# A chunked delta rule on TensorE: chunks of 128 tokens, one head per product, against chunks of 64 tokens, four heads in step

## The chip, the cores and the metric

The kernel runs on one core of a Trainium2 chip. The metric is device time in microseconds (us); the figure for the kernel before is the median of three executions. A core has a matrix engine (TensorE, in the profile PE, with its weight loads as PEld), VectorE (DVE), ScalarE (ACT), GpSimd (POOL) and SyncE (SP), which here issues DMAs. Products accumulate in PSUM, whose banks hold 128 x 512 floats; everything else that is on chip lies in SBUF.

## The reference

One block of a language model for 512 tokens and a model width of 1024, in float32: a projection of the normalised input, two mixers (a gated delta rule with 8 heads, `dk` = 128 and `dv` = 256, and a retention with 4 heads), their gates, an output projection and an MLP of width 4096. The change concerns the delta rule:

```python
CHUNK = 64
g_cum = jnp.cumsum(g, axis=-1)
decay = jnp.exp(jnp.where(causal, g_cum[..., :, None] - g_cum[..., None, :], -jnp.inf))
lower = jnp.where(strict, jnp.einsum('bhncd,bhnmd->bhncm', k * beta[..., None], k) * decay, 0.0)
t_inv = lax.linalg.triangular_solve(lower, eye, left_side=True, lower=True, unit_diagonal=True)
u = jnp.einsum('bhncm,bhnme->bhnce', t_inv, v * beta[..., None])
w = jnp.einsum('bhncm,bhnmd->bhncd', t_inv, k * beta[..., None] * jnp.exp(g_cum)[..., None])
attn = jnp.where(causal, jnp.einsum('bhncd,bhnmd->bhncm', q, k) * decay, 0.0)
q_exp = q * jnp.exp(g_cum)[..., None]
k_dec = k * jnp.exp(g_last - g_cum)[..., None]
def step(state, inp):                       # one chunk; scanned over the sequence
    qe, ww, uu, aqk, kd, ld = inp
    v_new = uu - ww @ state
    o = qe @ state + aqk @ v_new
    state = state * ld + kd.T @ v_new
    return state, o
oa = rmsnorm(o, norm_a) * silu(za)
ya = oa @ w_br_a
```

The length of a chunk is a choice of the algorithm and changes nothing but rounding: the kernel before uses 128 tokens, the reference 64.

## The kernel before

**Products.** The large projections run in F32R, TensorE's faster format for 32-bit data. Each operand is split into a high and a low part, and a product is taken as three (high by high, high by low, low by high). Weights come by DMA in pieces of 512 KB and are split in SBUF by ACT (high part, L148) and DVE (low part, L149). The small products of the delta rule are plain F32, for which the profile shows two passes each. For part of the projections a scheme with seven products of quarter matrices in place of eight is used. It needs sums of weight blocks, which small background DMA jobs prepare while the kernel runs; `REST` and two more constants say by the program's own reckoning from when and how often such a job is issued, and a sum that isn't done when it is wanted is issued there and then.

**Layout of the delta rule.** `kf` and `qf` hold keys and queries with features on partitions, `kd` keys with tokens on partitions, `dall` the decays (later the attention matrix), `rt` the inverse of the triangular matrix, `vt` the values with tokens on partitions. A tile holds 128 tokens of one head, so nearly every product uses the whole array of 128 x 128.

**Stages of the delta rule.** `key_tile` finishes the keys of a head; `keys_chain` multiplies keys by keys and scales by the gates; `base_inverse` inverts blocks of 32 x 32 on DVE; `double_blocks` (L1080 to L1173) grows them to 64 and then to 128 with products in parts of the array: its helper `abreast` interleaves two or three streams of products that sit in different quadrants. `recurrence(g2)` (L1323) handles two heads. For each of four chunks it runs, with two products of 256 columns each: `ks` (keys by state), `qs` (queries by state), `px` (inverse by corrected values), `pc` (keys by new values, which updates the state) and `po` (attention by new values). Between them DVE corrects the values (L1339) and updates the state (L1364), and ACT scales out of PSUM (L1355). Four such pairs of heads follow each other. `gate_chain` then applies norm and gate to the outputs, transposes them and splits them for the product with `w_br_a` (`ya_filler`). `late_gates_filler` computes half of the gates by the seven-product scheme, with tokens on partitions.

**What sets the order.** The class `Clock` (L659 to L735) plans the program in advance. *Fillers* are the projections (values, queries, gates, `ya`), cut into pieces of a few products; *chains* are the steps above. A chain gives up control with the time after which it should go on (`KS_US`, `PX_US`, `PC_US` and others), and the planner puts filler pieces there until that time is reached by its own reckoning. Every product of this stage goes through `clock.matmul` (L668) or `clock.transpose` (L677), which pin it in program order, so the order on TensorE is exactly the planned one and a product that waits holds back all behind it. DVE and ACT work is ordered by priorities (`REC_PRIO`, `OUT_PRIO`).

**Banks.** The projections use four PSUM banks (`mm`), the transposes one, and the chains share a ring of three:

```python
def chain_bank():
    return psx.tile([P, 4, P], F32, tag="dl", name="dl", bufs=3)
```

The functions that the change touches, before it:

## Time and profile before

| | |
|---|---|
| median of three executions | 1327.68 us (1327.45 to 1330.72) |
| the profiled execution | 1326.62 us, its span 1324.8 us |
| PE busy | 1308.9 us, 99% |
| PEld busy | 1085.9 us, 82% |
| DVE busy | 931.3 us, 70% |
| ACT busy | 668.7 us, 50% |
| POOL busy | 89.7 us, 7% |
| granted clock of TensorE | 0.999 |

How to read the profile. Times are microseconds of one execution. A line such as `L668 PE MATMUL dl<-vt,kd 128*128 128x256 f32 x48 | 12.5, 383` names the source line, the engine, the operation, output and inputs by their names in the program, for TensorE the part of the array used (128*128 is all of it, rows by columns), the shape, the type and the number of instructions, then busy time and mean nanoseconds of one; what follows is idle time ahead of them and what ended it. In a timeline a line begins with start and duration. Matmuls are pipelined and their ends are modelled, so durations overlap; distances between starts are the safer figure.

### The profile page before, as it was taken

Reading aid. Unit: us, or ns where it says so; the run is one execution under the profiler, and the core shown is the slowest. Engines: PE = TensorE matmul, PEld = TensorE weight load, DVE = VectorE, ACT = ScalarE, POOL = GpSimd, SP = SyncE. Lnnn points to the kernel's source line nnn. Section 1 sums busy time; section 2 is a strip of 40 time slices with the busy share of each in tenths; the row PEclk is TensorE's granted clock in tenths of the full one; section 3 lists DMA queues with packets and bytes.
Section 4 is the critical chain, followed back from the end, with each engine's and each line's share of the span. In section 5 each row is a group of like instructions: output and inputs, shape, how many; then the busy total and the mean of one; then the engine's idle time right before and its main releaser. Section 6 shows DMA issues by size and latency. Waiting matters only on the chain.

```text
span 1324.8 us, 17530 instructions
## 1 busy us (share of the span) xinstructions
PE 1308.9 (99%) x6591; PEld 1085.9 (82%) x6591; DVE 931.3 (70%) x1560; ACT 668.7 (50%) x1168; POOL 89.7 (7%) x95
## 2 busy tenths in 40 slices
PE   9999999999999999999999999999999999999997
PEld 7888787888888878888888888888889888888886
DVE  6889757486666578876567776789685746637478
ACT  5784546455534533544453443465266636355364
POOL 2100100000000001000010000000001000000001
PEclk9999999999999999999999999999999999999999
DMA  5336952476765568887293462545629895859635
GB/s 192 134 112 160 203 132 64 114 181 174 191 161 133 127 178 179 271 253 153 79 260 105 120 214 64 160 157 175 223 82 247 230 256 156 245 154 251 191 119 135
DMA packets 115557, 223.16 MB, mean 168 GB/s; under 512 B 6982, under 2 KB 38896, under 8 KB 114960
## 3 DMA queue, kind: packets, MB, share of 16 engines
q1 hardware_dynamic: 96496, 175.13, 41.3%
q0 software_dynamic: 16944, 40.54, 19.1%
q10 hardware_dynamic: 2032, 6.36, 1.3%
q8 instruction: 52, 0.85, 0.3%
q14 instruction: 33, 0.27, 0.1%
HBM read 216.75 MB, written 72.37 MB: 218 GB/s over the span
## 4 chain that ended last, share of the span: by engine, by line
PE 89%; DVE 6%; ACT 3%; issue 1%; DMA 1%; DVEq 0%; ACTq 0%
PE mm L668 18%; PE mm L317 17%; PE dl L317 11%; PE mm L93 10%; PE mm L95 10%; PE mm L94 10%; PE dl L668 5%; PE tr L397 1%; DVE wlo L149 1%; PE dl L94 1%; PE dl L95 1%; PE dl L93 1%; PE tr L677 1%; PE mm L632 1%; DVE tmp L1061 1%
## 5 line engine op out<-in xcount | busy, mean ns | idle before, releaser
L149 DVE TENSOR_TENSOR wlo<-raw,whi 128x1024 fp32r<-128x1024 f32 x269 | 328.2, 1222 | 204.2 <-ACT whi L148 203.1
L148 ACT CAST whi<-raw 128x1024 fp32r<-128x1024 f32 x269 | 282.6, 1052 | 356.5 <-PE mm L668 71.7
L668 PE MATMUL mm<-actT,whi 128*128 128x512 f32 x448 | 144.5, 403 | 0.0
L317 PE MATMUL mm<-whi,xsum 128*128 128x512 f32 x384 | 120.6, 390 | 0.0
L95 PE MATMUL mm<-hn,wlo 128*128 128x512 f32 (+1 forms) x288 | 105.4, 366 | 0.0
L94 PE MATMUL mm<-hn,whi 128*128 128x512 f32 (+1 forms) x288 | 105.3, 366 | 0.0
L93 PE MATMUL mm<-hn,whi 128*128 128x512 f32 (+1 forms) x288 | 105.3, 366 | 0.0
L668 PEld LDWEIGHTS mm<-actT,whi 128*128 128x128 f32 x448 | 80.6, 188 | 14.8
L668 PE MATMUL mm<-actT,wlo 128*128 128x512 f32 x224 | 87.7, 392 | 0.0
L317 PEld LDWEIGHTS mm<-whi,xsum 128*128 128x128 f32 x384 | 71.8, 188 | 14.9
L317 PE MATMUL mm<-wlo,xsum 128*128 128x512 f32 x192 | 74.8, 390 | 0.0
L317 PE MATMUL dl<-whi,ffq 128*128 128x512 f32 x224 | 71.3, 389 | 0.0
L668 PE MATMUL mm<-whi,og 128*128 128x512 f32 x192 | 62.3, 397 | 0.0
L95 PEld LDWEIGHTS mm<-hn,wlo 128*128 128x128 f32 x288 | 54.3, 189 | 8.8
L93 PEld LDWEIGHTS mm<-hn,whi 128*128 128x128 f32 x288 | 54.3, 189 | 8.7
L94 PEld LDWEIGHTS mm<-hn,whi 128*128 128x128 f32 x288 | 54.3, 189 | 8.7
L668 PE MATMUL mm<-whi,actT 128*128 128x512 f32 x176 | 60.3, 405 | 1.0 <-DVE qf L906 1.0
L317 PE MATMUL dl<-whi,actT 128*128 128x512 f32 x192 | 61.1, 390 | 0.0
L317 PE MATMUL mm<-whi,ffq 128*128 128x512 f32 x192 | 60.9, 389 | 0.0
L1830 DVE TENSOR_TENSOR ffq<-r,ffq 128x512 fp32r<-128x512 f32 (+1 forms) x64 | 39.2, 621 | 28.0 <-ACT ffq L1830 27.9
L135 POOL DMA_DIRECT2D sums<-in_w_in_dram x28 | 32.6, 1164 | 359.8 <-DMA sums<-in_w_in_dram 359.8
L93 PE MATMUL mm<-actT,whi 128*128 128x512 f32 x128 | 51.5, 402 | 0.0
(394 smaller groups left out, 2839.4 us busy)
## 6 DMA issues: line engine op xcount, KB each, us to landing
raw<-in_w_in_dram SPq DMA_DIRECT2D x95, 512.0 KB, 4.9
raw<-sums SPq DMA_DIRECT2D x64, 512.0 KB, 4.4
raw<-in_w_up_dram SPq DMA_DIRECT2D x36, 512.0 KB, 7.2
sums<-in_w_in_dram SPq DMA_DIRECT2D x32, 512.0 KB, 5.2
sums<-in_w_down_dram SPq DMA_DIRECT2D x32, 512.0 KB, 6.9
sums<-in_w_in_dram POOLq DMA_DIRECT2D x28, 512.0 KB, 7.4
raw<-in_w_down_dram SPq DMA_DIRECT2D x24, 512.0 KB, 5.9
sums<-sums POOLq DMA_DIRECT2D x20, 512.0 KB, 8.5
```

What stands on the lines that cost most here:

```text
L93: nc.tensor.matmul(ps, lh, rh, start=first, stop=False)
L94: nc.tensor.matmul(ps, lh, rl, start=False, stop=False)
L95: nc.tensor.matmul(ps, ll, rh, start=False, stop=last)
L135: tc.keep_in_program_order(nc.gpsimd.dma_start(dst, src, accum_op=ALU.add))
L148: nc.scalar.copy(hi[:, :n], raw[:, :n])
L149: nc.vector.tensor_tensor(lo[:, :n], raw[:, :n], hi[:, :n], ALU.subtract)
L317: m = nc.tensor.matmul(pss[t], lhs[i // 2], rhs[i % 2], start=first and k + i == 0, stop=k + i == 5, skip_group_check=not first,)
L397: nc.tensor.transpose(ps, src, ident)
L632: pin(nc.tensor.matmul(first_keys[f][:, 256:512], ws[w][:, kk, :], xs[x][:, 2 * j + kk, 256:512], start=False, stop=kk == 1 and i == 2, sk ...
L668: m = tc.keep_in_program_order(nc.tensor.matmul(*args, **kwargs))
L677: tc.keep_in_program_order(nc.tensor.transpose(ps, src, ident if by is None else by))
L1830: return nc.scalar.copy(dst[0], r), nc.vector.tensor_tensor(dst[1], r, dst[0], ALU.subtract)
```

## The change

The delta rule now works in chunks of 64 tokens. A tile holds two heads (`v`) side by side, and a recurrence handles a *quad* of four heads (`u` and `v`) for eight chunks (`e`); there are two quads in place of four pairs, so 16 steps as before. Products of 64 tokens use half of the array (`ks`, `qs`, `pc`, keys by keys, queries by keys) or a quadrant of it (`px`, `po`), and `clock.abreast` now lets the planner count two or three of them as running at once. The inverse is needed for blocks of 64 only, so the doubling keeps one of its two rounds. Each of the five products of a step is now four instructions of 256 columns; `px`, `pc` and `po` are written to two PSUM banks each, and `chain_bank` is as before. The gates are computed with features on partitions (values and gates get the same layout, so the output of the recurrence is scaled, transposed and then multiplied by the gate): `late_gates_filler` has 256 columns per product where it had 512. The small gate chain is rewritten for halves. `forms_chain` splits the gated output, the order of the fillers is new, and the planner's times and `REST` are set anew. `attention_chain` (queries by keys) was part of `query_chain`.

```diff
-VT_US, KS_US, PX_US, PC_US, GATE_US, FEAT_US, INV_PRIO, CONV_PRIO, SMALL_PRIO, KEY_PRIO, DECAY_US, AHEAD, TR_US, REC_PRIO, OUT_PRIO, SUM_PRIO = 2.5, 2.4, 3.5, 2.4, 11.0, 1.0, 0, 600, 800, 600, 20.0, 700, 2.2, 900, 900, 300
+FORM_US, FORM_PRIO, CONV_BUFS = 2.5, 300, 2
+VT_US, KS_US, PX_US, PC_US, GATE_US, FEAT_US, INV_PRIO, CONV_PRIO, SMALL_PRIO, KEY_PRIO, DECAY_US, AHEAD, TR_US, REC_PRIO, OUT_PRIO, SUM_PRIO = 2.5, 1.8, 2.4, 2.2, 4.5, 1.0, 0, 600, 800, 600, 20.0, 700, 2.2, 900, 900, 300
 DFF = 4096
-REST = 860.0, 985.0
+REST = 798.0, 923.0
...
+        def abreast(self, n):
+            before = self.now
+            yield
+            self.now = before + (self.now - before) / n
...
+            for v in range(2):
+                pk = psx.tile([P, 8, 64], F32, tag="dl", name="dl", bufs=3)
+                with clock.abreast(2):
+                    for e in range(8):
+                        for u in range(2):
+                            kc = key(q, u, v, e)
+                            clock.matmul(pk[halves[u], e, :], kc, kc, start=True, stop=True)
+                n = 16 * q + 8 * v
+                m = mt[:, n : n + 8, :]
                 with tc.high_priority(KEY_PRIO):
...
+            def bank():
+                return psx.tile([P, T], F32, tag="dl", name="dl", bufs=3).rearrange("p (n c) -> p n c", c=32)
+            def streams(*parts):
+                for i, step in enumerate(zip(*parts)):
+                    if i and i % 8 == 0:
                         yield 0.01
+                    with clock.abreast(len(parts)):
+                        for args in step:
+                            clock.matmul(*args, start=True, stop=True)
+            def first(q, u):
+                lo, hi = blocks[2 * u], blocks[2 * u + 1]
+                return [(p1[q][hi, n, :], mt[lo, 16 * q + n, 32:64], rn[lo, 16 * q + n, :]) for n in range(16)]
+            def left(q, u):
+                hi, out = blocks[2 * u + 1], []
+                for v in range(2):
+                    for e in range(8):
+                        n = 8 * v + e
+                        out.append((p2[u][blocks[2 * v], 8 * q + e, :], ys[q][hi, n, :], wide[hi, 16 * q + n, :]))
+                return out if u else out[8:] + out[:8]
+            p1 = [bank() for _ in range(2)]
+            yield from streams(first(0, 0), first(1, 1))
+            yield 0.01
+            yield from streams(first(0, 1), first(1, 0))
...
+        def attention_chain(q):
+            for u in range(2):
+                yield f"q{2 * q + u}"
+            yield "mt1"
+            for v in range(2):
+                pk = psx.tile([P, 8, 64], F32, tag="dl", name="dl", bufs=3)
+                with clock.abreast(2):
+                    for e in range(8):
+                        for u in range(2):
+                            clock.matmul(
+                                pk[halves[u], e, :], key(q, u, v, e), qfs[2 * q + u][:, e, halves[v]],
+                                start=True, stop=True,
+                            )
+                at = dall[q][:, 8 * v : 8 * v + 8, :]
                 with tc.high_priority(KEY_PRIO):
                     nc.vector.tensor_tensor(at, pk, at, ALU.mult)
                 yield clock.vector(0.7, 0.2) + VT_US
...
-                    for t in range(2):
-                        tt = slice(t * P, (t + 1) * P)
+                    for f in range(4):
                         for kk in range(2):
                             k = 2 * ks + kk
-                            for q in range(3):
+                            w = [v[:, kk, f * P : (f + 1) * P] for v in (wh, wl)]
+                            for j in range(3):
                                 clock.matmul(
-                                    pss[t], (xh, xl)[q // 2][:, k, tt], (wh, wl)[q % 2][:, kk, :],
-                                    start=first and k + q == 0, stop=k + q == 5, skip_group_check=not first,
+                                    pss[f % 2][:, f // 2].rearrange("p e t -> p (e t)"), w[j // 2], (xh, xl)[j % 2][:, k, :],
+                                    start=first and f // 2 + k + j == 0, stop=k + j == 5, skip_group_check=True,
...
+        def recurrence(q):
+            sso = pa2.tile([P, 2, 8], F32, tag="sso", name="sso")
+            state = pa2.tile([P, 2, 2, 256], F32, tag="st", name="state")
+            vt, qf = ([w[2 * q + u] for u in range(2)] for w in (vts, qfs))
+            every = [(u, v) for u in range(2) for v in range(2)]
+
+            def half_bank():
+                return chain_bank().rearrange("p c w -> p (c w)")[:, 0:256]
+
+            def pair_bank():
+                return chain_bank().rearrange("p (a c) w -> p a (c w)", a=2)
+
+            for e in range(8):
+                k, j = divmod(e, 4)
+                vx = [w[:, :, e, :] for w in vt]
+                n1 = [16 * q + 8 * u + e for u in range(2)]
+
+                def two(w):
+                    return w.rearrange("p (c w) -> p c w", c=2)
+
+                if e:
+                    ks = pair_bank()
+                    with clock.abreast(2):
+                        for u, v in every:
+                            clock.matmul(
+                                ks[halves[v], u, :], key(q, u, v, e), state[:, u, v, :], start=True, stop=True
+                            )
                     with tc.high_priority(REC_PRIO):
+                        for u in range(2):
                             nc.vector.scalar_tensor_tensor(
+                                vx[u], two(ks[:, u, :]), neg_eg[:, n1[u] : n1[u] + 1], vx[u], ALU.mult, ALU.add
                             )
                     t1 = clock.now
+                    qs = pair_bank()
+                    with clock.abreast(2):
+                        for u, v in every:
+                            clock.matmul(
+                                qs[halves[v], u, :], qf[u][:, e, halves[v]], state[:, u, v, :], start=True, stop=True
+                            )
                     yield KS_US - (clock.now - t1)
+                px = [half_bank() for _ in range(2)]
+                with clock.abreast(3):
+                    for u, v in every:
+                        clock.matmul(
+                            px[v][halves[u], :], rt[q][halves[v], 8 * u + e, :], vx[u][halves[v]], start=True, stop=True
+                        )
+                vn = pa2.tile([P, 2, 256], F32, tag="vn", name="vn")
                 with tc.high_priority(REC_PRIO):
+                    for v in range(2):
+                        n = 16 * q + 8 * v + e
+                        nc.scalar.activation(vn[:, v, :], px[v], AF.Copy, scale=br[:, n : n + 1])
+                if e:
+                    with tc.high_priority(OUT_PRIO):
+                        for u in range(2):
+                            nc.scalar.activation(vx[u], two(qs[:, u, :]), AF.Copy, scale=eg[:, n1[u] : n1[u] + 1])
                 yield PX_US
+                if e < 7:
+                    pc = [pair_bank() for _ in range(2)]
+                    with clock.abreast(2):
+                        for v in range(2):
+                            for u in range(2):
+                                clock.matmul(
+                                    pc[u][:, v, :], kd[q][halves[u], 7 * v + e, :], vn[halves[u], v, :],
+                                    start=True, stop=True,
+                                )
                     with tc.high_priority(REC_PRIO):
+                        if e:
+                            for v in range(2):
+                                for u in range(2):
+                                    n = 16 * q + 8 * v + e
+                                    nc.vector.scalar_tensor_tensor(
+                                        state[:, u, v, :], state[:, u, v, :], egl[:, u, n : n + 1], pc[u][:, v, :],
+                                        ALU.mult, ALU.add,
+                                    )
                         else:
+                            nc.vector.tensor_copy(state[:, 0], pc[0])
+                            nc.scalar.copy(state[:, 1], pc[1])
                 t1 = clock.now
+                po = [half_bank() for _ in range(2)]
+                with clock.abreast(3):
+                    for v in range(2):
+                        for u in range(2):
+                            clock.matmul(
+                                po[u][halves[v], :], dall[q][halves[u], 8 * v + e, :], vn[halves[u], v, :],
+                                start=True, stop=True,
                             )
                 with tc.high_priority(OUT_PRIO):
+                    for u in range(2):
+                        if e:
+                            nc.vector.tensor_tensor(vx[u], vx[u], two(po[u]), ALU.add)
+                        else:
+                            nc.vector.tensor_copy(vx[u], two(po[u]))
+                for u in range(2):
                     junk = sm.tile([P, 480], BF16, tag="junk", name="junk", bufs=1)[:, :256].rearrange("p (a n) -> p a n", a=2)
+                    nc.scalar.activation(junk, vx[u], AF.Square, accum_out=sso[:, u, e : e + 1])
                 yield PC_US - (clock.now - t1)
+                if j == 3:
+                    clock.start(gate_chain(q, k, sso))
...
+        def gate_chain(q, k, sso):
...
+            for u in range(2):
+                g2 = 2 * q + u
+                yield f"z{g2}"
+                for d in range(2):
+                    yield from clock.bank()
+                    ps = token_bank()
+                    for j in range(4):
+                        clock.transpose(ps[:, j, :], vts[g2][:, d, 4 * k + j, :])
+                    clock.tr = clock.now + TR_US
+                    z = zzs[g2][d][:, 4 * k : 4 * k + 4, :]
+                    nc.vector.scalar_tensor_tensor(z, ps, na[:, d : d + 1], z, ALU.mult, ALU.mult)
+                    yield FEAT_US
+                clock.done(f"gz{g2}{k}", FEAT_US)
+
+        def forms_chain(g2):
+            for k in range(2):
+                yield f"gz{g2}{k}"
+            yield (None, "ya0", "gz31", "ya1")[g2] if g2 else 0.0
+            zz = zzs[g2]
+            if g2 == 2:
+                og = [pa2.tile([P, 4, T], F32R, tag="vt", name="og", bufs=2) for _ in range(2)]
+            else:
+                og = [act.tile([P, 4, T], F32R, tag="og", name="og") for _ in range(2)]
+            ogs[g2] = og
             for f in range(4):
+                z = zz[f % 2][:, :, halves[f // 2]]
+                hi, lo = (w[:, f, :].rearrange("p (e t) -> p e t", t=64) for w in og)
+                with tc.high_priority(FORM_PRIO):
+                    nc.scalar.copy(hi, z)
+                    ya_marks.append(nc.vector.tensor_tensor(lo, z, hi, ALU.subtract))
+            clock.done(f"form{g2}")
+            clock.done(f"og{g2}", FORM_US)
...
                 (value_filler(0), ()),
-                (query_filler(0), ()),
+                (value_filler(1), ()),
                 (gate_filler(0), ()),
-                (value_filler(1), ()),
-                (query_filler(1), ()),
+                (gate_filler(1), ()),
+                (value_filler(2), ()),
+                (query_filler(2), ()),
+                (query_filler(3), ("quad0",)),
+                (value_filler(3), ("gz11",)),
                 (ya_filler(0), ("og0", "doubled")),
-                (value_filler(2), ("og0",)),
-                (query_filler(2), ()),
-                (gate_filler(1), ("gate0",)),
+                (late_gates_filler, ("sums", "form1")),
                 (ya_filler(1), ("og1",)),
-                (value_filler(3), ("og1",)),
-                (query_filler(3), ("og1",)),
-                (late_gates_filler, ("gate1",)),
                 (ya_filler(2), ("og2",)),
             ]
         )

```

636 lines of the change are left out of this document (278 added, 358 removed).

## The prediction

> **What bounds the kernel now.** I read the page first: busy time, then the busy time of the stretch in which the delta rule runs (41 to 465 us), then the chain of waits.
>
> ```profile
> span 1324.8 us, 17530 instructions
> PE 1308.9 (99%) x6591; PEld 1085.9 (82%) x6591; DVE 931.3 (70%) x1560; ACT 668.7 (50%) x1168; POOL 89.7 (7%) x95
> ```
>
> ```profile
> 41.00:465.00 424.00, 419.48 (x2382) 345.70 (x2382) 301.58 (x629) 228.25 (x515) 35.00 (x33) 1.00 0.58 144
> ```
>
> ```profile
> 264.50 29.29 PE mm L668 x129
> ```
>
> In the stretch row the numbers after the length 424.00 are PE, weight loads, DVE, ACT and POOL. TensorE is busy in 419.48 of 424 us, at the full granted clock (1.00); DVE idles for 122 us and ACT for 196. So the change gains what it takes off PE, at most 4.5 us of idle beside that, and loses whatever makes PE wait; DVE and ACT work costs nothing until PE stands for it. The chain row gives PE's beat: 29.29 us for 129 products of 512 columns in F32R, 0.227 us each. I price everything else by how far it pushes the next F32R product off that beat. The profiled execution took 1326.62 us, 1.8 more than its span and 1.1 less than the median 1327.68; sums are made against 1326.6.
>
> **What the old delta rule costs on PE.** First plain F32 products on the full array (timeline of PE, start and duration; a product shows as two passes):
>
> ```profile
> 183.96 0.39 PE L668 MATMUL mm<-actT,wlo 128*128 128x512 f32 x1
> 184.19 1.02 PE L668 MATMUL dl<-vt,kd 128*128 128x256 f32 x4
> 185.05 1.03 PE L668 MATMUL dl<-vn,dall 128*128 128x256 f32 x4
> 185.73 0.81 PE L668 MATMUL mm<-actT,whi 128*128 128x512 f32 x2
> 186.38 0.39 PE L668 MATMUL mm<-actT,wlo 128*128 128x512 f32 x1
> ```
>
> ```profile
> L668 PE MATMUL dl<-vn,dall 128*128 128x256 f32 x64 | 17.2, 386 | 0.8 <-ACT vn L1355 0.6 <-DVE dall L1214 0.2
> L668 PE MATMUL dl<-vt,kd 128*128 128x256 f32 x48 | 12.5, 383 | 0.0
> L668 PE MATMUL dl<-kf 128*128 128x128 f32 x64 | 8.5, 276 | 0.1
> ```
>
> From 183.96 to 186.38 are 2.42 us; three F32R products take 0.68, so four products of 256 columns take 1.74: 0.435 each, and entering and leaving costs nothing. The rows with x64 and x48 passes are 32 and 24 products; by the code `px` runs as often as `po` (`vn,dall`), `ks` and `qs` as often as `pc` (`vt,kd`), and queries by keys as often as keys by keys (`kf`). The recurrence: 2 x 32 + 3 x 24 = 136 products, 59.2 us. The 64 products of 128 columns at half the price: 13.9.
>
> Now the doubling of the inverse, the one place where the old kernel uses parts of the array (timeline of PE; 32*32 and 64*64 are the parts, and "..." hides passes that alternate in the same group):
>
> ```profile
> 143.20 0.39 PE L668 MATMUL mm<-actT,wlo 128*128 128x512 f32 x1
> 143.52 0.69 PE L668 MATMUL dl<-rn,acc 32*32 32x32 f32 x32
> 144.15 0.73 PE L668 MATMUL mm<-actT,whi 128*128 128x512 f32 x2
> 144.72 0.39 PE L668 MATMUL mm<-actT,wlo 128*128 128x512 f32 x1
> ```
>
> ```profile
> 152.47 0.40 PE L668 MATMUL mm<-actT,wlo 128*128 128x512 f32 x1
> 152.80 0.22 PE L668 MATMUL dl<-rt,mrb 32*32 32x32 f32 x2
> ...
> 153.17 0.73 PE L668 MATMUL mm<-actT,whi 128*128 128x512 f32 x2
> 153.75 0.39 PE L668 MATMUL mm<-actT,wlo 128*128 128x512 f32 x1
> ```
>
> ```profile
> 167.78 0.39 PE L668 MATMUL mm<-actT,wlo 128*128 128x512 f32 x1
> 168.10 0.27 PE L668 MATMUL dl<-rn,acc 64*64 64x64 f32 x1
> ...
> 169.18 0.73 PE L668 MATMUL mm<-actT,whi 128*128 128x512 f32 x2
> 169.75 0.40 PE L668 MATMUL mm<-actT,wlo 128*128 128x512 f32 x1
> ```
>
> ```profile
> 174.48 0.39 PE L668 MATMUL mm<-actT,wlo 128*128 128x512 f32 x1
> 174.80 2.07 PE L668 MATMUL dl<-rt,mrb 64*64 64x64 f32 x32
> 176.80 0.73 PE L668 MATMUL mm<-actT,whi 128*128 128x512 f32 x2
> 177.37 0.40 PE L668 MATMUL mm<-actT,wlo 128*128 128x512 f32 x1
> ```
>
> A visit is what PE spends on such a group between two F32R products: the distance of the outer rows less 0.68. Two streams of 32 columns, 16 products: 1.52 less 0.68 = 0.84. Three streams, 12 products: 0.60. Sixteen products of 64 columns in two streams: 1.29; in one stream: 2.21. Scaled from 0.435, a product of 64 columns streams in 0.109 us: one stream needs 1.74, two abreast 0.87. So streams in different quadrants do run abreast, and each visit has 0.42 to 0.47 us on top (0.40 for 32 columns). Three streams would stream in 0.22 and leave 0.38: they too are abreast, two of them on the same rows of the array. By the code the doubling makes 4 visits of 0.84, 8 of 0.60, 2 of 1.29 and 2 of 2.21: 15.2 us.
>
> **The change, part by part, on PE.** The nearest row for a visit of column parts alone is the 128*32 group in the gate chain:
>
> ```profile
> 49.03 0.40 PE L668 MATMUL mm<-actT,wlo 128*128 128x512 f32 x1
> 49.36 0.41 PE L668 MATMUL dl<-cmat,scratch 128*32 128x128 f32 x2
> 49.70 0.41 PE L668 MATMUL dl<-scratch,cmat 128*128 128x32 f32 x2
> ```
>
> 0.67 us, less 0.227 and 0.217 of streaming: 0.23 for the visit. The new shapes (128x64, 64x128, 64x64 with 256 columns) don't occur, so a visit lies between 0.23 and 0.45; I take 0.33.
>
> (1) Recurrence. Eight steps of two quads. `ks`, `qs` and `pc` are 14 groups each of four products, two abreast: 42 x 0.87 = 36.5. `px` and `po` are 16 groups each in four quadrants; three abreast is what the rows show, so 4 x 0.435 / 3 = 0.58 (0.435 with four, 0.87 with two): 18.6. Visits: `ks` with `qs` 14, `px` 16, `pc` with `po` 14 and `po` alone 2, together 46 x 0.33 = 15.2, and 14 changes of shape between `pc` and `po` at 0.1 (0 to 0.2): 1.4. Sum 71.7 against 59.2: **+12.5**. The products got cheaper by 4.1; the visits, which full-array groups don't have, cost 16.6.
>
> Where the Trainium skill bears on this: its page TensorEngine Tiling, section Tiling Modes, says that changing the tiling mode drains the array. It gives no price; the trace agrees, with 0.40 to 0.47 us a visit. Were there no drain, this term would be 4.1 less than before instead of 12.5 more.
>
> (2) Keys by keys and queries by keys: 8 visits of 16 products of 64 columns in two halves, 0.87 + 0.33 each: 9.6 against 13.9, **-4.3**.
>
> (3) Doubling: `first` and `left` are 4 visits each of 16 products in two streams, 8 x 0.84 = 6.7 against 15.2, **-8.5**.
>
> (4) Late gates: by features the 168 products of 512 columns become 336 of 256. Their beat:
>
> ```profile
> 26.59 5.99 PE L632 MATMUL mm<-actT,keep 128*128 128x256 f32 x48
> 32.42 2.05 PE L619 MATMUL pba<-actT,whi 128*32 128x256 f32 x16
> ```
>
> 5.83 us for 48, 0.1215 each: 40.8 against 38.1, **+2.7**. The early gates, values, queries and all transposes keep their number.
>
> (5) The gate chain's 16 products by the identity and six small ones in place of 4 and 3: three visits, **+1**.
>
> Work on PE: **+3.4 us**.
>
> **The new wait.** `chain_bank` still has three banks of PSUM (L786). Before, a step held `ks`, `qs`, `px`, then `pc` and `po`, one bank each. Now `px`, `pc` and `po` take two each. After `pc` the three banks hold `pc[0]`, `pc[1]` and what `qs` left; `po[0]` gets that one, and `po[1]` has to wait until `pc[0]` is read out, which the third of four state updates on DVE does. `po` stands right behind `pc` with no filler between, PE's order is written out, and behind `po` wait all fillers. How fast DVE answers, from the old step (one bank, two updates):
>
> ```profile
> 340.07 1.02 PE L668 MATMUL dl<-vt,kd 128*128 128x256 f32 x4
> ...
> 341.13 0.87 DVE L1364 SCALAR_TENSOR_TENSOR st<-st,egl,dl 128x256 f32<-128x256 f32 x2
> ```
>
> The first update starts 0.04 us after the last pass into its bank has ended (not after the first product), and the pair takes 0.87, the second 0.40 behind the first. New `pc`: four products stream in 0.87, DVE starts at about 1.07 after the group's start, and the third update ends at 1.07 + 0.87 + 0.40 = 2.34. The second `po` product would have started at about 0.97: PE loses **1.4 us** a step. Twelve steps have this (16.8); in the first step of each quad DVE and ACT copy instead, between 0 and 1.4, taken as 0.8 (1.6); the last has no `pc`. Sum **+18.4**. Lower end 0, if another bank is free; upper end with a weight split in DVE's way each time, 1.2 us by the row below: 14 x 2.6 = 36.
>
> ```profile
> L149 DVE TENSOR_TENSOR wlo<-raw,whi 128x1024 fp32r<-128x1024 f32 x62 | 75.7, 1221 | 43.0 <-ACT whi L148 42.9
> ```
>
> **Costed at nothing.** The other waits of a step: `KS_US`, `PX_US` and `PC_US` shrink by 0.2 to 1.1 us, but DVE's two updates (0.87 + 0.2) and ACT's two copies fit in them with fillers of three products (0.68) in front; uncovered, a weight split in the way costs up to 1.2 us each. DVE gets 32 more state updates net (0.40 each, 13 us), ACT the scaling of the gates; both have the idle time above. The four broadcasts and selects in place of two lie under the first fillers. `REST` moves 62 us ahead in the kernel's own reckoning, so some 7 jobs of 8.5 us fewer stand done at a given place of the program; what is missing is issued at need. Hidden by the weights split ahead; uncovered it is one such job, 10.7 us:
>
> ```profile
> sums<-in_w_down_dram POOLq DMA_DIRECT2D x16, 512.0 KB, 10.7
> ```
>
> **Sum.** 1326.6 + 3.4 + 18.4 = 1348.4 us, forecast **1348**; with 0.7 to 2.6 us of wait a step in place of 1.4, and the work as it stands, 1340 to 1366.
>
> **Rivals.** *Faster*: the bank wait isn't there and visits are cheap. Then quadrants run four abreast (-4.7), 54 visits cost 0.23 (-5.4) and the change inside a group nothing (-1.4): 3.4 - 11.5 = -8.1, 1318 (1314 if the stretch's 4.5 us of idle went too). For it: the three streams on shared rows, the 128*32 visit. Against it: three banks for four tiles. It decides where the mean wait of a `po` falls under 0.6 us. *No change*: work as summed, the wait gone because a bank comes free before `po[1]` asks for it: 1326.6 + 3.4 = 1330. The stretch's idle time speaks for it (PE could wait here in place of elsewhere), the count of banks against it. *The halves don't run abreast*: 128x64 products of 256 columns go one after the other, +28 x 0.87 + 8 x 0.87 = 31, and the quadrants only two at a time, +9: 1388. Against it the three streams, two of them on the same rows.
>
> **Chances.** Forecast 0.50, faster 0.28, no change 0.14, halves one by one 0.08. A difference under 0.3% (4 us) can't be told from no change. Faster takes its case and a little of the third: 0.30; the third leaves 0.10 within 4 us; the rest is slower, 0.60. The range 1314 to 1366 leaves out the fourth case and the thin ends of the first two.
>
> **What would show it.** Right: PE idle for over 1 us behind nearly every `pc`, waiting for DVE's state update; the groups of a step with their visits near 4.9 us (0.87 + 0.87 + 0.33, 0.58 + 0.33, 0.87 + 0.58 + 0.33 + 0.1) besides that wait; the doubling near 7 us; PE's share in the stretch falling from 99% to about 95%. Wrong: `po` following `pc` at once; rows of 128*64 whose passes don't overlap; PE waiting for weights or sums instead, late in the kernel; the stretch shorter than before.

## The result, and the profile after it

The changed kernel takes 1380.8 us (median of four, 1379.5 to 1385.4) against 1327.9 for the kernel before; the ratio is 1.040, with a 95% interval of 1.037 to 1.043. That is 53 us slower, where 20 were forecast and 1366 was the upper end of the range. The profiled execution of the changed kernel took 1385.4, and all sums on its trace below are against its span.

The page of the changed kernel: span, busy time by engine, and two rows of the forty slices (TensorE's busy share and its granted clock in tenths).

```profile
span 1383.3 us, 18549 instructions
...
PE 1332.0 (96%) x7049; PEld 1075.4 (78%) x7049; DVE 933.3 (67%) x1575; ACT 672.7 (49%) x1209; POOL 89.8 (6%) x106
...
PE   9899599999998999999999999999999999999997
...
PEclk9999679999999999999999999999999999999999
```

The span grew by 58.5 us. Of these, 23.1 are more busy time of TensorE (1332.0 against 1308.9), and 35.4 are time in which it is not busy (51.3 against 15.9). The largest part of both stands in one place: the fifth slice of PE has a 5 where the old page has a 9, and the fifth and sixth of the clock row have a 6 and a 7. So the next view is the busy time by stretch around 150 us, first of the changed kernel and then of the one before (after the length: PE, weight loads, DVE, ACT, POOL, and behind them the granted clock).

```profile
100.00:148.10 48.10, 46.13 (x264) 37.34 (x262) 45.54 (x131) 23.71 (x58) 4.14 (x4) 0.96 0.63 163
148.10:163.60 15.50, 0.04 (x3) 0.01 (x2) 15.19 (x60) 3.04 (x8) 1.06 (x2) 0.58 0.85 174
163.60:188.30 24.70, 24.70 (x291) 17.72 (x292) 5.01 (x8) 9.04 (x20) 1.79 (x2) 0.50 0.33 65
188.30:480.00 291.70, 277.08 (x1723) 203.02 (x1722) 175.82 (x333) 135.07 (x293) 16.82 (x15) 0.99 0.50 123
```

```profile
100.00:144.40 44.40, 43.38 (x236) 35.78 (x235) 43.89 (x152) 17.24 (x36) 5.04 (x5) 1.00 0.72 170
144.40:188.30 43.90, 43.63 (x554) 33.56 (x554) 26.27 (x36) 22.80 (x39) 5.12 (x5) 1.00 0.78 173
```

In the changed kernel TensorE stands for 15.5 us while DVE is busy for 15.19 of them. Then it works for 24.7 us at a granted clock of 0.50. Half of that, 12.3, would be lost if everything took twice as long; the starts below show some 10.4. From 188 to 480 us, where the recurrence runs, it is idle for 14.6 of 291.7. The second fence has the row that should have been read before the prediction: from 100 to 144 us DVE was busy for 43.89 of 44.40 us already in the kernel before.

What TensorE waited for most between 41 and 480 us (total, number of waits, longest):

```profile
PE dl L660 <- DVE big L1107: 15.5, 1, 15.5
PE dl L660 <- DVE state L1432: 12.0, 12, 1.8
PE dl L675 <- ACT f L1028: 3.6, 1, 3.6
PE tr L675 <- ACT junk L944: 2.0, 1, 2.0
```

L1107 is the last transpose of the base inverse; what waits is the first product of the doubling. L1432 is the state update, the wait that was forecast. The stall in the timeline of PE (start and duration):

```profile
147.74 0.39 PE L660 MATMUL mm<-actT,wlo 128*128 128x512 f32 x1
163.59 1.07 PE L660 MATMUL dl<-big,acc 32*32 32x32 f32 x32 [15.46 <-DVE big L1107]
164.58 1.22 PE L660 MATMUL mm<-actT,whi 128*128 128x512 f32 x2
165.60 0.63 PE L660 MATMUL mm<-actT,wlo 128*128 128x512 f32 x1
166.16 1.06 PE L660 MATMUL dl<-big,acc 32*32 32x32 f32 x32
...
187.46 0.63 PE L660 MATMUL mm<-actT,wlo 128*128 128x512 f32 x1
187.88 0.81 PE L660 MATMUL mm<-actT,whi 128*128 128x512 f32 x2
```

From 187.46 to 187.88 one F32R product takes 0.42 us instead of 0.227. The half clock is not only in the records, the beat has it too. A group of the doubling with its three F32R products takes 2.57 us (163.59 to 166.16), where the prediction's row of the kernel before has 1.52: less than twice. Eight such groups and ten more products at the slow beat make 8 x 1.05 + 10 x 0.2 = 10.4 us.

The inverse is late for more than one reason. The first is the length of its steps: DVE's groups while the 31 dependent steps run, in the kernel before (101.8 to 140.1 us) and in the changed one (111.5 to 159.8 us). L906 and L932 are the convolutions, L1104 is half of the inverse's own instructions.

```profile
L906 DVE SCALAR_TENSOR_TENSOR qf<-mm,convw,qf 128x511 f32<-128x511 f32 (+2 forms) x6 | 4.5, 742 | 0.0
L906 DVE SCALAR_TENSOR_TENSOR vt<-mm,convw,vt 128x511 f32<-128x511 f32 (+2 forms) x3 | 2.3, 754 | 0.0
```

```profile
L932 DVE SCALAR_TENSOR_TENSOR conv<-mm,convw,conv 128x509 f32<-128x509 f32 (+2 forms) x19 | 14.1, 741 | 0.3 <-ACT conv L929 0.3
L1104 DVE TENSOR_TENSOR mrb<-mrb,tmp 128x110 f32<-128x110 f32 (+35 forms) x59 | 13.2, 247 | 0.1
```

The old order of fillers is values, queries, gates, values, queries; the new one is both queries, both values, and then the gates, which bring DVE no convolution. So 19 convolution instructions stand between the steps of the inverse instead of 9. The planner counts the inverse as 46 us in both kernels.

The second is its start. The first step, in the timeline of DVE, before and after:

```profile
103.42 0.27 DVE L1061 TENSOR_TENSOR tmp<-mrb 128x16 f32<-128x16 f32 x2
```

```profile
112.08 0.26 DVE L1096 TENSOR_TENSOR tmp<-mrb 128x16 f32<-128x16 f32 x2
```

The steps begin 8.7 us later and end at 159.8 instead of 140.1, so they take 47.7 us instead of 36.7. Two transposes follow, and the first product of the doubling needs one of them. In the kernel before that one comes first (L1070, done at 142.5); in the changed one it comes second (L1107, done at 163.5), which holds the product for the 1.8 us of L1106 as well.

### The profile page after: what moved, and what is told of

Read it like the earlier page. It is cut to its first block, busy times and chain, and to the rows that moved or that the text cites. A ratio compares the mean times of both kernels' runs of the same rounds, so it can differ in the third digit from the quotient of the medians.

```text
span 1383.3 us, 18549 instructions
## 1 busy us (share of the span) xinstructions
PE 1332.0 (96%) x7049; PEld 1075.4 (78%) x7049; DVE 933.3 (67%) x1575; ACT 672.7 (49%) x1209; POOL 89.8 (6%) x106
## 4 chain that ended last, share of the span: by engine, by line
PE 85%; DVE 6%; ACT 5%; DMA 2%; issue 1%; DVEq 0%; ACTq 0%
PE mm L660 20%; PE mm L318 15%; PE mm L95 10%; PE mm L94 10%; PE mm L96 10%; PE dl L318 8%; PE dl L660 5%; DMA raw<-sums 2%; DVE wlo L150 1%; PE dl L94 1%; PE dl L96 1%; PE dl L95 1%; PE tr L398 1%; ACT whi L149 1%; PE tr L675 1%
## 5 line engine op out<-in xcount | busy, mean ns | idle before, releaser
L660 PE MATMUL mm<-actT,whi 128*128 128x512 f32 (+1 forms) x672 | 211.7, 400 | 0.0
L660 PEld LDWEIGHTS mm<-actT,whi 128*128 128x128 f32 x672 | 122.9, 196 | 31.9 <-issue 11.5
L660 PE MATMUL mm<-actT,wlo 128*128 128x512 f32 (+1 forms) x336 | 130.2, 387 | 0.0
L660 PEld LDWEIGHTS mm<-actT,wlo 128*128 128x128 f32 x336 | 66.0, 196 | 12.9
L932 DVE SCALAR_TENSOR_TENSOR conv<-mm,convw,conv 128x511 f32<-128x511 f32 (+2 forms) x72 | 53.0, 743 | 8.5 <-ACT conv L929 7.8
```

Of the source, the lines that this page charges most:

```text
L660: m = tc.keep_in_program_order(nc.tensor.matmul(*args, **kwargs))
L932: nc.vector.scalar_tensor_tensor(y[:, s:T], ps[:, 0 : T - s], tap(j), y[:, s:T], ALU.mult, ALU.add)
```

## The experiments

All times are medians; the kernel before took 1326.4 to 1328.0 beside them. The first four runs were made to tell the forecast wait from the late inverse.

**The inverse planned longer.**

```diff
-SMALL_US, CONV_US, TOK_US, PK_US, INV_US, DB_US = 10.5, 6.5, 2.5, 2.0, 46, 1.2
+SMALL_US, CONV_US, TOK_US, PK_US, INV_US, DB_US = 10.5, 6.5, 2.5, 2.0, 62, 1.2
```

> The planner is told that the base inverse takes 62 us instead of 46; nothing is computed differently, fillers (products of the gates) stand where the doubling stood. Theory 1 (the changed kernel's largest loss is one stall: TensorE stands 15.5 us at 148 us for the inverse on DVE, and then runs at half the granted clock until 188 us, 24.7 us after it has work again, which costs 12.3): both go, the granted clock is 1.00 from 148 to 188, the time is 1381 - 28 = 1353, 1350 to 1358. Rival 1 (the half clock is in the records but cost nothing): 1381 - 15.5 = 1365. Rival 2 (the products moved there are missing later as cover, so that what is saved comes back as waits behind the doubling): 1370 to 1381.

Measured: 1374.7, ratio 1.036 (1.034 to 1.037), 6 us less than the changed kernel. That is the second rival's range. The waits of this run:

```profile
PE dl L660 <- DVE state L1432: 12.8, 12, 1.8
PE dl L660 <- DVE big L1107: 7.0, 1, 7.0
PE tr L675 <- ACT vt L1474: 4.1, 1, 4.1
```

The stall shrank from 15.5 to 7.0 us only: the inverse now ended at 171.7 us instead of 163.5, because the products put ahead of it brought DVE more work: 26 convolutions and 9 weight splits stood between its steps instead of 19 and 6. And a wait of 4.1 us came up later. Planning a time longer helps little where the work put in between loads the engine that one waits for.

**Another bank for the second tile of `po`.**

```diff
-                po = [half_bank() for _ in range(2)]
+                yield from clock.bank()
+                po = [half_bank(), token_bank().rearrange("p c w -> p (c w)")[:, 0:256]]
+                clock.tr = clock.now + 1.5
```

> The second tile of po takes the bank of the transposes in place of the third chain bank; order of the products the same but for small shifts. Theory 1 (po[1] waits for pc[0] at every step; pc with po takes 3.28 us between F32R beats where 1.71 would do, 1.57 a step): 14 x 1.57 = 22 less, 1359, 1355 to 1363, and no idle time of over 0.3 us between pc and po. Rival 1 (what is lost is the idle time that the profile shows behind pc, 12.9 us in 14 gaps): 1368. Rival 2 (the wait is for something else, such as the new values or the attention matrix, or it moves to the transposes' bank): within 4 of 1381.

Measured: 1357.7, ratio 1.023 (1.021 to 1.025): 23 us less, as the first theory has it. One `pc` with `po` in the timeline of PE, in the changed kernel and in this one, and behind it `ks` with `qs` and `px`:

```profile
233.90 0.39 PE L660 MATMUL mm<-actT,wlo 128*128 128x512 f32 x1
234.22 1.71 PE L660 MATMUL dl<-vn,f 64*128 64x256 f32 x10
236.70 0.66 PE L660 MATMUL dl<-vn,f 64*64 64x256 f32 x6 [0.78 <-DVE state L1432]
237.28 0.73 PE L660 MATMUL mm<-actT,whi 128*128 128x512 f32 x2
237.86 0.39 PE L660 MATMUL mm<-actT,wlo 128*128 128x512 f32 x1
```

```profile
226.33 0.39 PE L660 MATMUL mm<-actT,wlo 128*128 128x512 f32 x1
226.65 1.49 PE L660 MATMUL dl<-vn,f 64*128 64x256 f32 x9
...
228.31 0.73 PE L660 MATMUL mm<-actT,whi 128*128 128x512 f32 x2
228.88 0.39 PE L660 MATMUL mm<-actT,wlo 128*128 128x512 f32 x1
...
230.25 0.39 PE L660 MATMUL mm<-actT,wlo 128*128 128x512 f32 x1
230.57 1.08 PE L660 MATMUL dl<-state,f 128*64 128x256 f32 x8
231.48 1.03 PE L660 MATMUL dl<-state,qf 128*64 128x256 f32 x8
232.45 0.73 PE L660 MATMUL mm<-actT,whi 128*128 128x512 f32 x2
233.02 0.39 PE L660 MATMUL mm<-actT,wlo 128*128 128x512 f32 x1
...
233.71 0.39 PE L660 MATMUL mm<-actT,wlo 128*128 128x512 f32 x1
234.03 0.66 PE L660 MATMUL dl<-vt,f 64*64 64x256 f32 x8
...
235.19 0.40 PE L660 MATMUL mm<-actT,wlo 128*128 128x512 f32 x1
```

The outer rows of `pc` with `po` are 3.96 us apart with the wait (233.90 to 237.86) and 2.55 without (226.33 to 228.88), so it costs 1.41 us in this step, where the profile shows only 0.78 of idle time: the modelled end of the product ahead covers the rest.

**The inverse ahead of the convolutions on DVE.** Only the constant `INV_PRIO` changes, from 0 to 900.

> The base inverse's DVE work gets a higher priority than the convolutions (900 in place of 0); the planned order of TensorE is as in the changed kernel. Theory 1 (the inverse is late because convolutions and weight splits of four projections are put in front of its 31 dependent steps on DVE: 51 us from 112 to 163 where the kernel before took 37 from 103 to 140): it ends at about 145, the 15.5 us of stall and the half clock behind it go; what the convolutions now wait holds the four projection banks for up to 30 us and gives some of it back: 1355 to 1370. Rival (its own chain of steps sets the inverse's length, not what is put in between): it ends within 3 us of 163 again and the time is within 6 of 1381.

Measured: 1368.7, ratio 1.031 (1.030 to 1.033), 12 us less, at the upper end of the first theory's range. But the inverse ended at 157.8 us, where the theory had 145: its steps began at 114.3, and they took 38.9 us with 18 convolutions still between them. So this run doesn't show that the convolutions are the cause. The stall before the doubling went because TensorE itself came to it later, at 160.4, after waits of which the longest new ones are below; the long half clock went too, but 0.62 was granted between 92 and 101 us.

```profile
PE dl L675 <- ACT kd L1028: 6.6, 1, 6.6
...
PE tr L675 <- ACT vt L939: 3.1, 1, 3.1
```

The priority also holds for ACT's copies into the inverse, and the keys' scaled copies (L1028) wait behind them. In the first run below that takes the priority from the first of these copies, the wait for the keys is gone.

**One entry of the order of fillers moved.**

```diff
-                (value_filler(1), ()),
                 (gate_filler(0), ()),
+                (value_filler(1), ()),
```

> One entry of the order of fillers is moved: the first gates' products come before the second values, so that the projections in the inverse's window bring DVE fewer convolutions (four tiles of three instructions, some 9 us); the planner is also allowed to go on when only waiting fillers are left. Theory 1 (DVE's convolutions delay the inverse): it ends 7 to 9 us earlier, the stall at about 148 us shrinks from 15.5 to some 7 us, the clock still drops but for less: 1381 - 8 - 0 to 6 = 1367 to 1373. Rival (the inverse's length is its own): 1381 within 5, or more, as values are ready later.

Measured: 1407.7, ratio 1.061 (1.059 to 1.062): 27 us more. The rival allowed for more, as values are ready later, but gave no size, and it had the inverse unchanged. The inverse did end 4.5 us earlier (159.0), less than the 7 to 9 of the first theory, and the stall was 10.4 us. But the second values are needed by the recurrence, which started 12 us later (218.7 instead of 206.3) and ended 23 us later, when no filler was left. Behind its end (granted clock behind the POOL column):

```profile
502.00:517.00 15.00, 11.01 (x30) 7.16 (x30) 7.91 (x12) 6.61 (x14) 1.14 (x1) 0.50 0.28 48
```

So the new order has a reason: what the recurrence needs must come before it, and that is just what loads DVE.

**Fewer convolutions in the inverse's time.**

```diff
-            for j in (2, 1, 0):
+            for j in (2,) if ch < 4 or 16 <= ch < 24 else (2, 1, 0):
```

> Leaves out two of the three multiply-adds of the convolution on DVE, for the queries and values of the first four heads only (12 tiles, 24 instructions of 0.65 us, 15.6 us of DVE inside the inverse's window). TensorE's order is that of the changed kernel. Theory 1 (DVE is the engine that sets the end from 100 to 163 us; what is put in front of the inverse there makes it late): the inverse ends some 12 to 16 us earlier, the stall at 148 us falls from 15.5 to under 4, the half clock behind it goes or shrinks to one window of 3.4 us: 1381 - 12 - 10 = 1359, 1352 to 1363. Rival 1 (the inverse's own chain of 31 steps sets its length): 1381 within 5. Rival 2 (as with the longer planned inverse, what is saved comes back as new waits later): 1370 to 1377.

Measured: 1369.2, ratio 1.031 (1.029 to 1.032), 12 us less. DVE's convolutions in the inverse's time, in this run:

```profile
L932 DVE SCALAR_TENSOR_TENSOR conv<-mm,convw,conv 128x511 f32<-128x511 f32 x6 | 4.5, 744 | 0.0
```

With 6 of them instead of 19 the inverse ended at 153.3, 10 us earlier, and the stall fell to 5.4 us. The steps took 36.4 us, as in the kernel before (36.7), where the changed kernel took 47.7. This is shown, then: DVE's other work makes the steps long. They still began at 111.3, so the later start is another part of the stall; no run here takes it alone, nor the order of the two transposes, and what each is worth stays open. The time is above the range of the first theory mainly because half clock still followed the shorter stall, for 13.7 us.

**Two edits together, and a third.** The bank for `po` and the priority; then also the token bank for the last of four groups of key transposes.

> Two edits together: the second tile of po in the transposes' bank, and the inverse ahead of the convolutions on DVE. Theory 1 (the waits behind pc and the late inverse are two separate losses in different stretches): the two gains add, 1381 - 23 - 12 = 1346, 1343 to 1350. Rival (they are one queue of waits; the earlier chain runs out of fillers): 1352 to 1358.

> As the two edits together, and the last of the four groups of key transposes of a quad takes the transposes' bank in place of a fourth turn in the ring of three. Theory 1 (TensorE's 0.95 and 3.6 us at 57 to 62 us are waits for a chain bank that ACT still reads with sums of squares and scaled copies, and the half clock behind them costs 1.7): 4 to 7 us less than with the two edits, about 1341. Rival (ACT is busy there without a break, so the wait moves to the next product): within 2 of the two edits, 1346.

Measured: 1347.2, ratio 1.014 (1.013 to 1.016), and 1343.9, ratio 1.012 (1.010 to 1.013). The first two gains add (1381 - 23 - 12 = 1346), so they are separate losses. The third edit brought 3 us of the 4 to 7 expected; the wait of 3.6 to 3.9 us for L1028 went, and of the 6.6 us for ACT's key copies 4.7 stayed.

**The background jobs' times back to 860 and 985.**

> The changed kernel with the background jobs' two times as they were before (860 and 985 in place of 798 and 923). Theory 1 (they follow the planner's own reckoning, which ends 62 us earlier, and cost nothing): 1381 within 4. Rival (fewer jobs stand done, sums are issued at need; one such job is 10.7 us): over 4 us off, in either direction.

Measured: 1381.8, ratio 1.040 (1.038 to 1.042). No difference: they cost nothing, as the prediction had it.

**Planning by the traces.** All four runs start from the three edits together. Two put the transposes of values and queries later and take the priority from ACT's first copies; two more also plan the inverse and the outputs' transposes later. The diff shows the main lines of the first.

```diff
-            yield clock.vector(2.1, 0.9) + CONV_US
+            yield clock.vector(2.1, 0.9) + CONV_US + 3.5
...
-            with tc.high_priority(INV_PRIO):
-                for q in range(2):
+            for q in range(2):
+                with tc.high_priority(INV_PRIO * q):
```

> The three edits together (po in the transposes' bank, the inverse ahead on DVE, the last key group in the transposes' bank), and two more: the planner has the transposes of values and queries 3.5 us later behind their convolution, and ACT's copies of the first half of the blocks for the inverse lose their priority. Theory 1 (what is left over the kernel before, 1344 against 1327.6, is idle time and half clock: 16.8 us of gaps against 4.9, and half clock in three places): the gaps of 2.7, 3.0 and 0.7 us before transposes and most of the 4.7 at 83 us go, with the half clock behind them: 1344 - 10 to 14 = 1330 to 1334. Rival 1 (the smaller products cost more work, so that 1344 is near the floor): 1340 to 1344. Rival 2 (the values come too late for the recurrence): over 1344.

> As the run before, with 6 us in place of 3.5. Theory 1: within 3 of it, as 3.5 us are enough, 1328 to 1335. Rival (the transposes are still early by more than that): 3 to 6 less. Rival 2 (the chain of the recurrence starts later and its end lacks fillers): 3 to 10 more.

> The three edits together (po, inverse, keys) and the planner's waits set by what the traces show: 54 us for the inverse, 6.5 us more behind the convolution of a value, 3.5 behind that of a query, 8 in place of 4.5 us before the outputs' transposes; ACT's copies of the first blocks without priority. Theory 1 (the work on TensorE is within 4 us of the kernel before; all else that was lost is waits and the half clock behind them): gaps of some 6 to 9 us in all, no half clock at the doubling, 1327 to 1334. Rival 1 (the smaller products cost more, near the 12.5 us forecast for the recurrence): gaps go, and the time stays at 1338 or more. Rival 2 (every wait planned away comes back elsewhere, as DVE and ACT are the bound in this part): 1340 to 1350 with gaps of 13 us or more.

> As the run before, with 57 us for the inverse, 5 us for the values and 6 us before the outputs' transposes. Theory 1: within 4 of it. Rival 2 of the run before: the two differ by more than 5, as each setting only moves the waits.

Measured: 1344.4 (ratio 1.014, 1.012 to 1.016), 1351.4 (1.018, 1.017 to 1.020), 1347.4 (1.017, 1.013 to 1.021) and 1346.0 (1.014, 1.012 to 1.016). None gained on 1343.9. In the first, the longest wait that was left stood right ahead of the doubling, 3.8 us for a value on DVE, and the half clock lasted through the first half of the doubling, as the stretch behind it shows; from 155.8 us on the clock is 1.00. In the last, the transposes of the values waited 8.3 us for DVE.

```profile
139.80:155.80 16.00, 14.71 (x154) 10.78 (x155) 12.01 (x14) 8.86 (x20) 1.89 (x2) 0.50 0.82 136
```

```profile
PE tr L675 <- DVE vt L1197: 8.3, 1, 8.3
```

L1197 rescales the values; in these kernels it stands behind the inverse on DVE. The second rival of the first replanned run held, in time and in waits (17.7 us of them): the waits moved from product to product. The second replanned run came within 1.4 us of it, as its first theory had it.

**The groups of the doubling further apart.**

```diff
                     if i and i % 8 == 0:
-                        yield 0.01
+                        yield 5.0
```

The two other `yield 0.01` between groups became 5.0 as well.

> The changed kernel with the eight groups of small products of the doubling further apart: the planner puts 5 us of projection products between two groups in place of one piece of 0.7. The stall of 15.5 us before the first group stays. Theory 1 (half clock lasts because no window of 3.4 us behind the stall is filled by large products, the groups of 32 x 32 alternate with 0.7 to 1.3 us of them): the clock returns after the first such window, 4 to 10 us after TensorE has work again, and 7 to 10 us less is lost there; the recurrence starts some 10 us later, which may take some of it back: 1371 to 1378. Rival (after a stall of that length the clock stays down for some fixed time of 35 to 40 us): half clock until 185 to 190 us again, no gain, 1380 or more.

Measured: 1382.0, ratio 1.041 (1.039 to 1.043), no gain. But the clock did what the first theory says. The stretches behind the stall, in this run:

```profile
164.00:170.00 6.00, 4.93 (x41) 4.07 (x42) 1.01 (x1) 5.67 (x15) 2.00 (x2) 0.50 0.60 97
170.00:176.00 6.00, 6.00 (x54) 4.72 (x53) 1.23 (x1) 1.05 (x1) 0.00 (x0) 0.94 0.53 87
```

TensorE has work from 165.07; full clock is back about 6 us later, where the changed kernel, with groups after every three large products, needed 24.7. So no fixed time holds it down. Why the saving there, some 8 us by the beats above, didn't show in the time isn't settled; the doubling ended later, and two more short spells of half clock came up at 270 and 318 us.

**The rescaling ahead of the inverse, and then the second half of the doubling later.** The priority around L1197 goes from 600 to 950; then `DB_US` from 1.2 to 3.5.

> As the second replanned version, and the rescaling of the values on DVE goes ahead of the inverse (priority 950 against 900; before, 600). Theory 1 (the work is that of the kernel before within 3 us, and the rest is waits): the wait of 8.3 us at 139 us goes, with most of the half clock behind it: 1346 - 8 - 2 = 1336, 1333 to 1338. Rival (DVE is the bound from 100 to 145 us, and the wait returns before another product there): 1342 to 1347.

> As the run before with the rescaling first, and the planner waits 5.25 in place of 1.8 us between the two halves of the doubling. Theory 1 (work is equal within 3 us; what is left is waits and half clock): the 2.15 us before the second half and the 5.1 us of half clock behind it go: 1339 - 7 = 1332, 1330 to 1334. Rival (the wait moves, or some 12 us are the price of the smaller products): 1336 to 1341.

Measured: 1339.1, ratio 1.008 (1.006 to 1.011), and 1334.7, ratio 1.006 (1.004 to 1.008). Both gains came near the first theory's size (7 us for 10, 4.4 for 7), though each time is just above its range. The wait of 8.3 us went when DVE's order changed, so there it was this order that held the values, and not DVE's load as a whole. The page of the last:

```profile
span 1330.5 us, 18547 instructions
...
PE 1310.1 (98%) x7049; PEld 1062.4 (80%) x7049; DVE 930.8 (70%) x1575; ACT 672.2 (51%) x1209; POOL 90.8 (7%) x106
```

TensorE is busy for 1310.1 us against 1308.9 in the kernel before: the changed kernel's work is 1.2 us more. What the last version has over the kernel before beside that is idle time (20.4 us outside the busy time against 15.9). No version beat the kernel before.

## Why the prediction was wrong

**Work on TensorE: right in sum, with some luck.** The forecast was +3.4; measured +1.2 of busy time once most waits and all half clock of this stretch were gone. By parts, from distances between F32R products less 0.68 (the first three from the rows of the run with another bank, the last two from the run with two edits): `ks` with `qs` 2.09 (forecast 2.07), `px` 0.80 (0.91), `pc` with `po` without the wait 1.87 (1.88), a group of the doubling 0.83 (0.84), a group of keys by keys 1.29 (1.20). Halves run two abreast, as forecast. Quadrants run four abreast where three were forecast: with another bank, the four products of a pass of `po` start within 0.02 us of each other. Their streaming is then 0.435 instead of 0.58, and what is left for a visit is some 0.35 to 0.42 us instead of 0.33, or 0.56 for `pc` with `po` instead of 0.43. The two errors cancel, so the 1.87 for 1.88 is luck. The gain of the smaller products is eaten up by the visits. The rival nearest to the time, halves one by one at 1388, isn't what happened: `ks` with `qs` would have taken 8 x 0.435 and a visit, 3.8 us instead of 2.09.

**The bank wait: right.** The forecast was 1.4 us a step and 18.4 in all; 1.41 was measured in a step of the first quad, and 23 went when another bank was given. Mechanism and place hold, and the size nearly. By distances the fourteen steps lose some 21 us, since in the second quad the waits are longer (up to 1.8 us of visible idle time). The rest of the 23 is a spell of half clock behind one of them: the granted clock is 0.79 from 392 to 400 us in the changed kernel, and 1.00 from 188 to 480 with another bank.

**"Costed at nothing": this step failed.** It said that DVE and ACT "both have the idle time above", and that was an average over 424 us. In the 44 us in which the inverse runs DVE had 0.5 us to spare, in the kernel before already. The new order of fillers put ten more convolution instructions in front of the inverse's steps. Counted from start to start, they are 6.6 of the 11 us by which the steps got longer; the rest is the rescaling of values, small instructions and the inverse's own. The prediction priced the fillers by TensorE alone, where the order changes nothing. The later start of the inverse and the order of its two transposes were at nothing too. In the profiled execution the late inverse takes 15.5 us of stall and some 10.4 of half clock. Taking it away on the chip brought 12 us at first, and more only when the waits that came in its place went too.

**Not considered: half clock.** No term and no rival had a lower granted clock, since the kernel before shows 1.00 in the whole stretch. In the changed kernel each stall of 2 us or more has a price on top. The other stalls (3.6 and 2.0 us ahead of transposes, for ACT) and one window of half clock behind each, 1.7 us, add 9 us. With the terms as measured the sum is 1348.4 - 2.2 (work) + 4.6 (bank wait) + 25.9 + 9.0 = 1385.7, against 1385.4 for the profiled execution. It comes this close partly by chance: shorter waits, some 4 us in both kernels, are left out, and the 4.6 is from medians.

**What was to show it.** TensorE's share did fall, to 91% between 41 and 480 us where 95 was forecast, but the main idle time stood ahead of the doubling, not behind `pc`. Behind most `pc` the profile shows 0.78 us of idle time, not over 1; the distances have the 1.4. The groups of a step took 4.76 us (forecast 4.9). None of the signs of "wrong" that were named came; the early chain wasn't on the list. The rival "no change", at 1330, is near what the last repaired version took.

## What to carry to other kernels

A busy share is to be read in the stretch in which a moved piece of work will stand, for every engine that this piece uses: an engine with 30% to spare on average had 1% to spare where the order was changed. When the order of independent work is changed, list what each piece brings to the other engines, and which dependent chain runs there at that time. A stall right ahead of small, scattered products can cost more than its length: here the clock came back only within a longer run of large ones, and not in each.

## What the runs showed of the hardware

**The granted clock.** It is 1.00 or 0.50, and it fell behind gaps of TensorE as short as 2.0 and 1.6 us. Behind the gap of 2.0 us at 107 us (the wait for ACT's L944 above) the clock is lower in the next stretch of the changed kernel:

```profile
108.00:112.00 4.00, 2.78 (x10) 2.31 (x11) 4.00 (x4) 2.56 (x14) 0.20 (x1) 0.72 0.94 227
```

The gap alone doesn't decide: in the recurrence of the changed kernel the clock fell behind a gap of 1.58 us at 393 us (0.52 from 397 to 400), and not behind one of 1.82 us at 446 (1.00 from 446 to 460).

The spell at 108 us is about 3.4 us long, and in the doubling it lasted through 24.7 us of work, in which groups of 32 x 32 products alternate with runs of three to nine large ones. One such run of 4.1 us (172.30 to 176.44) didn't bring the clock back; 3.1 us into a later one it did. With the groups further apart it ended after some 6 us, 4.6 us into the first run of large products. The Trainium skill, page TensorE: Matmul & The Clock Gate, section Part 1: The HAM clock gate (the "warmup" mystery), says that the clock is released after a busy window of about 3.4 us; the run with the groups apart is in line with it, with 4.6 us of large products alone ahead of the return. The changed kernel isn't, if any busy time counts: PE is busy for 24.70 of 24.70 us behind the stall, at 0.50. The same page, section HAM oscillation — how this bites in real kernels, gives gaps of over some 3.4 us as what is to be avoided; here a gap of 2.0 us was followed by half clock, and the measurement decides.

**Hidden waits.** A wait of 1.41 us showed as 0.78 of idle time, because ends of matmuls are modelled. Distances between the starts of large products gave the full price.
